# Two running sums seeded in PSUM, a second weight sum by DMA, and seven products in another order

## The chip, the cores and the metric

The kernel runs on one core of a Trainium2 chip. The metric is the device time of one execution in microseconds (us); of several executions the median is given. Engines are named as in the profile: PE is the matmul engine (TensorE), with its weight loads in rows of their own (PEld); DVE is the vector engine, ACT the scalar engine, POOL the engine that also issues DMAs which add to their destination, SP the one that issues the weight loads from memory. PSUM is the memory that PE writes, in eight banks of 128 x 512 float32.

## The reference: what is computed

One decoder block on 256 positions of width 2048, in float32: a half-step SwiGLU layer (width 5632), a token mixer (a recurrent branch and a short convolution that share one input projection, with one output projection), a second half-step SwiGLU layer, and a last norm.

```python
def swiglu_ffn(x, w_gate, w_up, w_down):
    return (jax.nn.silu(x @ w_gate) * (x @ w_up)) @ w_down
...
x = x + FFN_RESIDUAL_SCALE * swiglu_ffn(rms_norm(x, ffn1_norm[l]), ffn1_w_gate[l], ffn1_w_up[l], ffn1_w_down[l])
z = rms_norm(x, mix_norm[l]) @ w_in[l]
...
x = x + y @ w_out[l]
x = x + FFN_RESIDUAL_SCALE * swiglu_ffn(rms_norm(x, ffn2_norm[l]), ffn2_w_gate[l], ffn2_w_up[l], ffn2_w_down[l])
return rms_norm(x, final_norm)
```

All time goes to the large matrix products; their weights are about 340 MB, each read once.

## The kernel before

**Split operands.** A float32 product is made from parts: each operand is split into a high part `hi` (the value cast to the matmul's reduced type `fp32r`, by ACT, in two halves) and a low part `lo` (what is left, by DVE, one subtraction). A weight tile `raw` is 128 x 4 x 512 (1 MB); `parts_of` (L214) makes its `hi` and `lo`. A product of one weight tile with one row half of the activations is 12 matmuls in `multiply` (L228): 8 with `hi` (activation high and low), then 4 with `lo`. A "plain" piece makes both row halves at once: 24 matmuls, 16 with `hi`, then 8 with `lo`. The split tiles rotate over three slots (`split_tiles`, L198), so a cast waits until PE has done with the high part of the piece three places earlier.

**Blocks of seven products.** `seven` (L417) multiplies a 2 x 2 arrangement of activation tiles with a 2 x 2 arrangement of weight tiles (`w11`, `w12`, `w21`, `w22`) by seven products instead of eight, with sums of weights and sums of partial results. Beside these it adds plain pieces for the other activation tiles: `b2`, `b3` for one column half, `a2`, `a3` for the other. Four PSUM banks are in use, `a`, `c`, `e` and `d`. The products are numbered 0, 4, 5, 6, 2, 3, 1 in the order before, called `p0`, `p4` and so on here. `p0` goes to bank `a`, on which `p5`, `p6`, `a2` and `p3` go on adding; `p4` goes to `c`. After `p0` and `p4` ACT copies the banks to tiles in the on-chip memory (`snap`: `s1`, `s5`), and after `p5` and `p6` the running state of `a` (`u2`, `u3`). When a result is complete, `done` adds the copies to its bank on DVE (`total`, L871). Weight sums that `p4`, `p5` and `p3` need are made in `w11` by DVE (128 x 2048 each, three in a block); the one for `p6` is made in `w12` by a DMA that POOL issues and that adds `w22` to it (L464).

The kernel runs 28 such blocks: gate and up blocks by turns for five pairs of columns in each SwiGLU layer (`gate`, `up`; L867 on), a down block after the first, third and fifth pair (`down`, L793, with plain products of `product` before and after it), one in the input projection (`in_c`) and one in the output projection (`o_q`). The first gate block (its order is written out by hand) and `o_q` have paths of their own. Names in the profile carry `g`, `u`, `d`, `in_c`, `o_q` for these: `lo_u_p` is the low part of a weight tile of one of the seven products of an up block, `hi_u_x` the high part of a plain piece, `ps_u_c` the bank `c` of an up block.

**What sets the order.** Nearly everything is recorded through one helper at L43. Outside the opening and the end the program's order isn't kept as written: when the program is built, a planner goes through it with a clock of its own, and gives each engine the first instruction, in the order of writing, whose operands it believes ready. On the chip each engine then runs its list strictly in that order. The planner also gives out the tiles' slots; the weight loads are issued by SP as buffers come free. `raw` tiles have three buffers, `w11` and `w12` two of their own. The banks rotate over eight slots, in the order in which `bank` (L85) is called.

Of the kernel before, what the change touches and what calls it, by code (L numbers as in the profile page):

```python
# [13 lines left out]
ALU = mybir.AluOpType  # L14
AX = mybir.AxisListType

P = 128
D = 2048
S = 256
FF = 5632  # L20
NT = S // P
KD = D // P
KF = FF // P
CW = 512
NC_D = D // CW
UK = 4
# [23 lines left out]
def hybrid_block(ctx: ExitStack, tc: tile.TileContext, a: dict, out: bass.AP):  # L50
    nc = tc.nc
# [30 lines left out]
    work = ctx.enter_context(tc.tile_pool(name="work", bufs=2, side="right"))  # L82
    psum = ctx.enter_context(tc.tile_pool(name="psum", bufs=8, space=bass.MemoryType.PSUM))

    def bank(name):  # L85
        return psum.tile([P, 512], F32, tag="ps", name=name)

    def f32(ap):
        return ap.bitcast(F32)
# [13 lines left out]
    early = const.tile([P, 1], F32, name="early")  # L103
    act.activation(early, ones[:, :1], AF.Sqrt)

    idle = bank("idle")

    def keep_busy(n):
        for _ in range(n):
# [6 lines left out]
    def load_vectors(group, name, engine, after=None):  # L116
        n = sum(g[2] for g in group)
        rows = const.tile([n, P], F32, name=f"rows_{name}")
        cols = const.tile([P, n], F32, name=f"cols_{name}")
        at = 0  # L120
        if after is not None:
            engine.tensor_copy(rows[:, :1], after[:n, :1])
        for key, ap, k in group:
            engine.dma_start(rows[at : at + k, :], ap.rearrange("(r p) -> r p", p=P))
            vec[key] = cols[:, at : at + k]
            at += k

        def turn():
            pv = bank(f"pv_{name}")
            pe.transpose(pv[:, :n], rows, ident[:n, :n])  # L130
            dve.tensor_copy(cols, pv[:, :n])

        return turn
# [115 lines left out]
    class Norm:  # L249
# [12 lines left out]

        def transposed(self, k, src, whole):

            pt = bank(f"pt_{self.name}_{k}")[:, :S]
            for t in range(NT):
                pe.transpose(pt[:, t * P : (t + 1) * P], src[t], ident)
            g = self.gain[:, k : k + 1]
            hi, lo = whole[:, k % UK, :S], whole[:, k % UK, S:]
            parts = [  # L270
                lambda: act.activation(hi, pt, AF.Copy, scale=g),
                lambda: dve.scalar_tensor_tensor(lo, pt, g, f32(hi), op0=ALU.mult, op1=ALU.subtract),
            ]
            if self.exact is not None and k < 2 * UK:
                v = self.exact[:, k % UK, k // UK * S : (k // UK + 1) * S]
                parts.append(lambda: act.activation(v, pt, AF.Copy, scale=g))
            return parts
# [28 lines left out]

        def rows(self):

            pb = bank(f"pb_{self.name}")
            for t in range(NT):  # L310
                pe.matmul(pb[:, t * P : (t + 1) * P], ones, self.diag[t], start=True, stop=True)
            self.bc = work.tile([P, S], F32, tag="bc", name=f"bc_{self.name}")
            dve.tensor_copy(self.bc, pb[:, :S])
# [38 lines left out]
    def product(w, c, us, y, name, stagger=False, between=None):  # L352
        ps = [bank(f"ps_{name}_{t}") for t in range(NT)]
        cs = slice(c * CW, (c + 1) * CW)
        late = []
        for i, u in enumerate(us):
            blk = unit(w[u * UK * P : (u + 1) * UK * P, cs], f"{name}_{u}")
            begin, end = i == 0, i == len(us) - 1
            if stagger and i >= len(us) - 2:
                late.append((u, blk, begin, end))  # L360
            else:
                multiply([(ps[t], stationary(y(u), t), begin, end) for t in range(NT)], blk)
            if between:
                between(i)
            pump(1.5)

        for t in range(NT):
            for i, (u, blk, begin, end) in enumerate(late):
                if t < NT - 1:
                    multiply([(ps[t], stationary(y(u), t), begin, end)], blk)  # L370
                elif not end:
                    multiply([(ps[t], stationary(y(u), t), begin, i == len(late) - 2)], blk)
                else:
                    for o in (slice(0, CW // 2), slice(CW // 2, CW)):
                        ps.append(bank(f"ps_{name}_last")[:, : CW // 2])
                        multiply([(ps[-1], stationary(y(u), t), True, True)], [(h[:, o], l[:, o]) for h, l in blk])
        return ps

# [38 lines left out]
    def seven(w, rows, cols, sf, xs, name, keep, done, between=None, early=False, own=None, factor=None):  # L417
# [14 lines left out]
        def get(u, n, kept=False):  # L432
            src = w[u * UK * P : (u + 1) * UK * P, cols[n] : cols[n] + CW]
            return load(src, f"{name}_{u}{n}", kept=kept)
# [2 lines left out]
        w11, w12 = get(r0, 0, True), get(r0, 1, True)  # L437
        b2, w22 = get(xs[0][0], 1), get(r1, 1)
        b3 = get(xs[1][0], 1) if two else None
        a2, w21 = get(xs[0][0], 0), get(r1, 0)  # L440
        a3 = get(xs[1][0], 0) if two else None

        def snap(ps, n, scale=1.0):
# [7 lines left out]
        def usual(i, raw, n, *targets, first=None):  # L451
# [6 lines left out]
            if own and last:  # L458
                for t in range(NT):
                    own(t, n, apart[t, n])  # L460

        product_of(0, w11, a, True)
        dve.tensor_tensor(w11, w12, w11, op=ALU.add)
        nc.gpsimd.dma_start(w12, w22, accum_op=ALU.add)  # L464
# [3 lines left out]
        blk = None  # L468
# [55 lines left out]
    def ffn(tag, norm, after, opening=False):  # L524
        with tc.tile_pool(name=f"ffn{tag}", bufs=1, side="left") as fp:
# [10 lines left out]
            def turn_hidden(u, t, h, again):  # L536

                if u not in hidden:
                    hidden[u] = big(f"h{tag}_{u}")
                pt = bank(f"ph{tag}_{u}_{t}")  # L540
                for j in range(UK):
                    pe.transpose(pt[:, j * P : (j + 1) * P], h[:, j * P : (j + 1) * P], ident)
                pt = pt.rearrange("p (j c) -> p j c", j=UK)
                hi = hidden[u][:, :, t * P : (t + 1) * P]
                lo = hidden[u][:, :, S + t * P : S + (t + 1) * P]
                act.copy(hi, pt)
                dve.tensor_tensor(lo, pt, f32(hi), op=ALU.subtract)
                if again:
                    act.copy(quad(h), pt)
                    turned[u, t] = quad(h)  # L550
# [242 lines left out]
            def down(last):  # L793
# [24 lines left out]
                for c in (0, 3):  # L818
                    end = last and tag == 2 and c == NC_D - 1
                    ps = product(  # L820
                        wd, c, us[:-2] + [n, m], hidden.get, f"d{tag}_{m}_{c}", end,
                        (lambda i: settle()) if c == 0 else None,
                    )
                    Engine.pinned = end
                    if end:
                        finish(c, ps)
                    else:
                        for t in range(NT):
                            update(c, t, ps[t])
                    if c == 0:  # L830
                        sh = {}
                        two, last_sum, high, low = seven_of(
                            sh, hidden[m], hidden[n],
                            {(t, i): turned[u, t] for t in range(NT) for i, u in ((0, m), (1, n))},
                            quad(keep(f"hspare{tag}_{m}")),
                            [[quad(keep(f"hs{tag}_{m}_{i}_{z}", F32R)) for z in range(2)] for i in range(4)],
                        )
                        two()
                        high(5)
                        low(5)  # L840

                        def others(i):
                            if i == "sum":
                                high(6)
                                low(6)
                                last_sum()
                                high(2)
                                low(2)

                        got = {}  # L850

                        def add(t, b, ps, tiles):
                            got[t, b] = [ps] + tiles
                            if (0, b) in got and (1, b) in got:
                                for i in range(NT):
                                    update(2 - b, i, *got[i, b])

                        if tag == 1 and m == 5:
                            prepare()
                        seven(  # L860
                            wd, (m, n), (2 * CW, CW), sh, [(u, hidden[u]) for u in us[:-2]], f"d{tag}_{m}", keep, add,
                            others,
                        )
# [106 lines left out]
    with tc.tile_pool(name="mixer", bufs=1, side="left") as mp, tc.tile_pool(name="mixw", bufs=2, side="left") as mw:  # L970
# [35 lines left out]
        def gates(q):  # L1006
# [4 lines left out]
            th = {}  # L1011
            for g, hb in (("a", hba), ("i", hbi)):
                hi, lo = wgate[g]
                pg = bank(f"pgate_{g}_{q}")
                pe.matmul(pg[:, :S], hi[:, q, :], xs[:, :S], start=True, stop=False)
                pe.matmul(pg[:, :S], hi[:, q, :], xs[:, S:], start=False, stop=False)
                pe.matmul(pg[:, :S], lo[:, q, :], xs[:, :S], start=False, stop=True)
# [124 lines left out]
        def sc_c(between):  # L1142
# [10 lines left out]
            def turn(n):  # L1153
                for f in range(0, 4, 2):
                    pt = bank(f"pt_c{n}_{f}")
                    for i in range(2):
                        for t in range(NT):
                            o = i * S + t * P
                            pe.transpose(pt[:, o : o + P], z[t, n][:, (f + i) * P : (f + i + 1) * P], ident)
                    for i in range(2):  # L1160
                        q = 4 * (1 - n) + f + i
                        c = tmp("cc", q, S + 2, bufs=8)
# [79 lines left out]
        for g in range(2):  # L1242
            if g == 1:
                flush()
            ps = product(w_out, 0, (2 * g, 2 * g + 1), yT.__getitem__, f"o0_{g}")
            pst = bank(f"pst_{g}")
            for t in range(NT):
                pe.matmul(pst[:, t : t + 1], acc[:, g, t * P : (t + 1) * P], ones[:, :1], start=True, stop=True)
            tot = work.tile([P, NT], F32, tag="tot", name=f"tot_y{g}")
# [155 lines left out]
```

## Time and profile before

| | |
|---|---|
| median of 3 runs | 1726.82 us (1726.74 to 1728.6) |
| the profiled execution: its own time | 1726.91 us |
| the profiled execution: span from first to last instruction | 1725.1 us |
| DVE, instructions and busy time | 1212, 1452.2 us |
| ACT, instructions and busy time | 1406, 1077.8 us |
| data read from memory | 339.82 MB |

A group or timeline row reads: line, engine, operation, written tile `<-` read tiles, partitions x elements, and the count; a timeline row begins with its start and its length in us, and ends with the idle time before it and what ended that. The waits view lists who waited for whom, in us, times, and the longest. A row by stretches gives the stretch, its length, the busy time of PE, PEld, DVE, ACT and POOL with their instruction counts, the granted matmul clock, the busy share of the DMA engines and GB/s. Matmuls overlap: a row's length is that of the pipeline, and the time that one costs is read from start to start.

### The profile page before, as it was taken

How to read it: one execution, taken by the hardware profiler on the slowest of the kernel's cores; microseconds unless marked ns; L12 is line 12 of the kernel's file. 1: busy time of each engine (PE TensorE's matmuls, PEld its weight loads, DVE VectorE, ACT ScalarE, POOL GpSimd, SP SyncE). 2: the span in 40 equal slices, each digit the busy share in tenths (PEclk: the TensorE clock that was granted, in tenths of full speed). 3: DMA queues.
4: the chain of work that ended last, by engine and by line, in shares of the span. 5: the costliest groups of instructions: out<-in, count | busy, mean ns of one | idle time of the engine just before them, and what ended most of it. 6: DMA issues, size and time to landing. Idle time of an engine off the chain costs nothing.

```text
span 1725.1 us, 20426 instructions
## 1 busy us (share of the span) xinstructions
PE 1715.3 (99%) x7985; PEld 1432.9 (83%) x7985; DVE 1452.2 (84%) x1212; ACT 1077.8 (62%) x1406; POOL 35.3 (2%) x62
## 2 busy tenths in 40 slices
PE   9999999999999999999999999999999999999998
PEld 8888888888888888888888888888888888888886
DVE  7988889789789888787897889889788887788886
ACT  7666566656466656666965657655556664556664
POOL 0010000000000000000000000000000000000000
PEclk9999999999999999999999999999999999999999
DMA  8775777667677766655556675776777757677753
GB/s 300 225 258 174 242 234 227 214 236 233 182 238 226 227 201 219 211 160 193 175 197 205 204 251 165 228 237 224 230 227 219 244 171 243 214 225 220 254 179 128
DMA packets 178256, 372.59 MB, mean 216 GB/s; under 512 B 6132, under 2 KB 9072, under 8 KB 174448
## 3 DMA queue, kind: packets, MB, share of 16 engines
q1 hardware_dynamic: 173632, 340.81, 58.4%
q0 software_dynamic: 4352, 29.43, 8.5%
q8 instruction: 62, 1.02, 0.2%
q10 hardware_dynamic: 176, 1.06, 0.2%
q14 instruction: 34, 0.28, 0.0%
HBM read 339.82 MB, written 2.10 MB: 198 GB/s over the span
## 4 chain that ended last, share of the span: by engine, by line
PE 99%; DVE 0%; ACT 0%; DVEq 0%; issue 0%; ACTq 0%
PE ps_d L43 14%; PE ps_in L43 10%; PE ps_g_a L43 9%; PE ps_u_a L43 9%; PE ps_g_c L43 6%; PE ps_u_c L43 6%; PE ps_d_a L43 5%; PE ps_u_d L43 5%; PE ps_g_d L43 5%; PE ps_d_c L43 3%; PE ps_u_e L43 3%; PE ps_g_e L43 3%; PE ps_g L43 3%; PE ps_o L43 3%; PE ps_u L43 3%; PE ps_d_d L43 3%
## 5 line engine op out<-in xcount | busy, mean ns | idle before, releaser
L43 ACT CAST hi_g_p<-raw_g 128x1024 fp32r<-128x1024 f32 (+1 forms) x139 | 142.1, 1054 | 111.6 <-DVE raw_g L43 26.9
L43 DVE TENSOR_TENSOR lo_g_p<-raw_g,hi_g_p 128x2048 fp32r<-128x2048 f32 x70 | 159.8, 2289 | 42.3 <-ACT hi_g_p L43 41.6
L43 DVE TENSOR_TENSOR lo_u_p<-raw_u,hi_u_p 128x2048 fp32r<-128x2048 f32 x70 | 159.3, 2288 | 39.5 <-ACT hi_u_p L43 39.2
L43 ACT CAST hi_u_p<-raw_u 128x1024 fp32r<-128x1024 f32 x140 | 141.3, 1047 | 70.1 <-issue 23.1
L43 PE MATMUL ps_d<-hi_d,h 128*128 128x512 f32 x696 | 166.0, 390 | 0.0
L43 PEld LDWEIGHTS ps_d<-hi_d,h 128*128 128x128 f32 x696 | 130.0, 188 | 26.6
L43 ACT CAST hi_d<-raw_d 128x1024 fp32r<-128x1024 f32 x88 | 88.6, 1048 | 68.3 <-PE ps_u_d L43 19.9
L43 DVE TENSOR_TENSOR lo_d<-raw_d,hi_d 128x2048 fp32r<-128x2048 f32 x44 | 100.8, 2290 | 29.3 <-ACT hi_d L43 29.3
L43 PE MATMUL ps_in<-xT_nm,hi_in 128*128 128x512 f32 x512 | 122.5, 391 | 0.0
L43 ACT CAST hi_d_p<-raw_d 128x1024 fp32r<-128x1024 f32 x84 | 85.2, 1048 | 59.2 <-DVE raw_d L43 33.7
L43 PEld LDWEIGHTS ps_in<-xT_nm,hi_in 128*128 128x128 f32 x512 | 94.0, 188 | 18.8 <-ACT tha L43 0.5
L43 DVE TENSOR_TENSOR lo_d_p<-raw_d,hi_d_p 128x2048 fp32r<-128x2048 f32 x42 | 95.5, 2288 | 15.5 <-ACT hi_d_p L43 15.4
L43 ACT CAST hi_g_x<-raw_g 128x1024 fp32r<-128x1024 f32 (+1 forms) x79 | 81.2, 1058 | 42.9 <-PE ps_g_c L43 25.6
L43 ACT CAST hi_u_x<-raw_u 128x1024 fp32r<-128x1024 f32 x80 | 80.5, 1046 | 36.4 <-PE ps_u_c L43 22.1
L43 DVE TENSOR_TENSOR lo_g_x<-raw_g,hi_g_x 128x2048 fp32r<-128x2048 f32 x40 | 91.5, 2288 | 9.2 <-ACT hi_g_x L43 8.9
L43 DVE TENSOR_TENSOR lo_in<-raw_in,hi_in 128x2048 fp32r<-128x2048 f32 x32 | 73.2, 2288 | 26.7 <-ACT hi_in L43 26.3
L43 DVE TENSOR_TENSOR lo_u_x<-raw_u,hi_u_x 128x2048 fp32r<-128x2048 f32 x40 | 91.4, 2286 | 1.4 <-ACT hi_u_x L43 0.8
L43 PE MATMUL ps_d<-lo_d,h 128*128 128x512 f32 x348 | 86.2, 389 | 0.0
L43 ACT CAST hi_in<-raw_in 128x1024 fp32r<-128x1024 f32 x64 | 64.0, 1045 | 24.9 <-PE ps_in L43 15.2
L43 PEld LDWEIGHTS ps_d<-lo_d,h 128*128 128x128 f32 x348 | 65.3, 188 | 13.6
L43 DVE TENSOR_TENSOR raw_u<-raw_u,raw_u 128x2048 f32<-128x2048 f32 x30 | 68.7, 2289 | 8.5 <-DMA raw_u<-in_ffn_w_up_dram 8.1
L43 DVE TENSOR_TENSOR raw_g<-raw_g,raw_g 128x2048 f32<-128x2048 f32 x30 | 68.7, 2289 | 5.7 <-DMA raw_g<-in_ffn_w_gate_dram 5.2
(477 smaller groups left out, 3750.5 us busy)
## 6 DMA issues: line engine op xcount, KB each, us to landing
raw_d<-in_ffn_w_down_dram SPq DMA_DIRECT2D x88, 1024.0 KB, 5.2
raw_u<-in_ffn_w_up_dram SPq DMA_DIRECT2D x87, 1024.0 KB, 5.3
raw_g<-in_ffn_w_gate_dram SPq DMA_DIRECT2D x86, 1024.0 KB, 5.2
raw_in<-in_w_in_dram SPq DMA_DIRECT2D x32, 1024.0 KB, 5.1
raw_g<-raw_g POOLq DMA_DIRECT2D x10, 1024.0 KB, 7.0
raw_u<-raw_u POOLq DMA_DIRECT2D x10, 1024.0 KB, 7.0
raw_in_c<-in_w_in_dram SPq DMA_DIRECT2D x8, 1024.0 KB, 5.3
raw_o<-in_w_out_dram SPq DMA_DIRECT2D x8, 1024.0 KB, 5.2
```

The lines of the kernel that those rows point to most:

```text
L43: ins = getattr(self.engine, name)(*args, **kwargs)
```

## The change

`bank` notes for each new bank whether the one that had the slot before it was written as a whole by PE (`fit`). In `seven`, the 26 blocks without a path of their own get a new sequence.

- `p2` is made right after `p5`, ahead of the piece `b3`; `p6` comes behind `b3`. To match, `w21` is loaded ahead of `a2`, and in the down blocks the activation sums for `p2` are made before those for `p6` (`others`).
- The third weight sum, `w21` added to `w11` for `p3`, is made by a DMA of POOL in place of DVE.
- Where the slots of `c` and `d` fit, which is so in 21 of the 26 blocks (10 of the first layer, 11 of the second; not in `in_c`, nor in the first up block of either layer, the fourth gate block of the first and the first gate block of the second), the sums are seeded: `p4` is made first, into `e`, and ACT copies `e` to `c`; then `p0` into `a`, and ACT copies `a` to `d`. PE goes on adding on both, so that the snapshots `s1` and `s5` and the two DVE adds that used them fall away. `p0`'s weight tile is still split first, since the first weight sum overwrites it.

The transposes of hidden tiles and of `pt_c` are written as matmuls with the transpose flag, of which only the first of a bank starts it (`turn_into`); their number is the same.

```diff
+    written = [False] * 8
+    given = [0]
+    fit = {}
+
+    def bank(name, whole=True):
+
+        slot = given[0] % len(written)
+        given[0] += 1
+        fit[name] = written[slot]
+        written[slot] = whole
         return psum.tile([P, 512], F32, tag="ps", name=name)
+
+    def turn_into(ps, sources):
+
+        for i, src in enumerate(sources):
+            pe.matmul(
+                ps[:, i * P : (i + 1) * P], src, ident, is_transpose=True, start=i == 0, stop=True,
+                skip_group_check=True,
+            )
...
-        a2, w21 = get(xs[0][0], 0), get(r1, 0)
+        if early or own:
+            a2, w21 = get(xs[0][0], 0), get(r1, 0)
+        else:
+            w21, a2 = get(r1, 0), get(xs[0][0], 0)
...
+        if not early and own is None:
+            first = parts_of(w11, f"{name}_p0")
+            dve.tensor_tensor(w11, w12, w11, op=ALU.add)
+            nc.gpsimd.dma_start(w12, w22, accum_op=ALU.add)
+            seeded = fit[f"ps_{name}_c"] and fit[f"ps_{name}_d"]
+            if seeded:
+                product_of(4, w11, e, True)
+                act.copy(c, e)
+                product_of(0, None, a, True, blk=first)
+                act.copy(d, a)
+                s1, s5 = [], []
+            else:
+                product_of(0, None, a, True, blk=first)
+                product_of(4, w11, c, True)
+                s1, s5 = [snap(a, "s1")], [snap(c, "s5")]
+            if between:
+                between(0)
+            usual(0, b2, 1, (e, 1, not seeded, not two), (c, 0, False, False))
+            if between:
+                between(1)
+            dve.tensor_tensor(w11, w22, w11, op=ALU.add)
+            if between:
+                between("sum")
+            product_of(5, w11, a)
+            nc.gpsimd.dma_start(w11, w21, accum_op=ALU.add)
+            u2 = snap(a, "u2", -1.0)
+            if between:
+                between(2)
+            product_of(2, w22, c, end=not two)
+            if two:
+                usual(1, b3, 1, (e, 1, False, True), (c, 0, False, True))
+            done(0, 1, c, [u2])
+            product_of(6, w12, a)
+            u3 = snap(a, "u3", -1.0)
+            done(1, 1, e, [u3] + s5)
+            usual(0, a2, 0, (d, 0, not seeded, False), (a, 1, False, False))
+            product_of(3, w11, a, end=not two)
+            if two:
+                usual(1, a3, 0, (a, 1, False, True), (d, 0, False, False))
+            done(1, 0, a, [])
+            product_of(1, w21, d)
+            done(0, 0, d, s1)
+            return
...
                         def others(i):
                             if i == "sum":
-                                high(6)
-                                low(6)
                                 last_sum()
                                 high(2)
                                 low(2)
+                            elif i == 2:
+                                high(6)
+                                low(6)
```

More of the change, by code (lines that the diff above doesn't have):

```diff
@@ L83, in hybrid_block @@
     psum = ctx.enter_context(tc.tile_pool(name="psum", bufs=8, space=bass.MemoryType.PSUM))
-    def bank(name):
-        return psum.tile([P, 512], F32, tag="ps", name=name)
+    written = [False] * 8
[6 more added lines that the diff above has]
+        written[slot] = whole
+        return psum.tile([P, 512], F32, tag="ps", name=name)
+    def turn_into(ps, sources):
[4 more added lines that the diff above has]
+            )
     def f32(ap):
@@ L104, in hybrid_block @@
     act.activation(early, ones[:, :1], AF.Sqrt)
-    idle = bank("idle")
+    idle = bank("idle", False)
     def keep_busy(n):
@@ L128, in turn @@
         def turn():
-            pv = bank(f"pv_{name}")
+            pv = bank(f"pv_{name}", False)
             pe.transpose(pv[:, :n], rows, ident[:n, :n])
@@ L263, in transposed @@
         def transposed(self, k, src, whole):
-            pt = bank(f"pt_{self.name}_{k}")[:, :S]
+            pt = bank(f"pt_{self.name}_{k}", False)[:, :S]
             for t in range(NT):
@@ L307, in rows @@
         def rows(self):
-            pb = bank(f"pb_{self.name}")
+            pb = bank(f"pb_{self.name}", False)
             for t in range(NT):
@@ L374, in product @@
                     for o in (slice(0, CW // 2), slice(CW // 2, CW)):
-                        ps.append(bank(f"ps_{name}_last")[:, : CW // 2])
+                        ps.append(bank(f"ps_{name}_last", False)[:, : CW // 2])
                         multiply([(ps[-1], stationary(y(u), t), True, True)], [(h[:, o], l[:, o]) for h, l in blk])
@@ L540, in turn_hidden @@
                 pt = bank(f"ph{tag}_{u}_{t}")
-                for j in range(UK):
-                    pe.transpose(pt[:, j * P : (j + 1) * P], h[:, j * P : (j + 1) * P], ident)
+                turn_into(pt, [h[:, j * P : (j + 1) * P] for j in range(UK)])
                 pt = pt.rearrange("p (j c) -> p j c", j=UK)
@@ L1013, in gates @@
                 hi, lo = wgate[g]
-                pg = bank(f"pgate_{g}_{q}")
+                pg = bank(f"pgate_{g}_{q}", False)
                 pe.matmul(pg[:, :S], hi[:, q, :], xs[:, :S], start=True, stop=False)
@@ L1155, in turn @@
                     pt = bank(f"pt_c{n}_{f}")
[L1156 to L1159, printed above, removed]
+                    turn_into(
+                        pt, [z[t, n][:, (f + i) * P : (f + i + 1) * P] for i in range(2) for t in range(NT)]
+                    )
                     for i in range(2):
@@ L1245, in hybrid_block @@
             ps = product(w_out, 0, (2 * g, 2 * g + 1), yT.__getitem__, f"o0_{g}")
-            pst = bank(f"pst_{g}")
+            pst = bank(f"pst_{g}", False)
             for t in range(NT):
```

## The prediction

> **What bounds the kernel now.** I read the page first: the busy line, the chain, then the waits of the matmul engine (PE), then one table by stretches.
>
> ```profile
> span 1725.1 us, 20426 instructions
> ...
> PE 1715.3 (99%) x7985; PEld 1432.9 (83%) x7985; DVE 1452.2 (84%) x1212; ACT 1077.8 (62%) x1406; POOL 35.3 (2%) x62
> ...
> PE 99%; DVE 0%; ACT 0%; DVEq 0%; issue 0%; ACTq 0%
> ```
> ```profile
> PE idle L43 <- DVE ones L43: 1.1, 1, 1.1
> PE ps_g L43 <- ACT hi_g L43: 0.6, 1, 0.6
> 18.00:1717.00 1699.00, 1698.90 (x7908) 1418.99 (x7907) 1439.16 (x1185) 1063.47 (x1377) 34.63 (x56) 1.00 0.67 215
> 1717.00:1725.10 8.10, 0.00 (x0) 0.00 (x0) 2.67 (x10) 1.63 (x4) 0.00 (x0) 0.79 0.48 179
> ```
>
> PE is busy 1698.9 of the 1699 us between 18 and 1717 us, at the full granted clock; its two waits, 1.7 us together, are in the opening. So only two things can move the end: fewer matmuls, or a new pause of PE. The change has exactly as many matmuls as before (seven products of 12 and four plain pieces of 24 in a block with two more inputs, and the same transposes). It takes work from DVE, for which PE waits at no place but the start, and brings some operands closer to their due time. The question is where an operand now comes late.
>
> Here is the seam between a gate block and its up block, the first of its kind. PE, rows of 8 and 4 matmuls (`p3` low, `p0` high, `p0` low, `p4` high; then `p5`, `a2`, and `p3` low again):
>
> ```profile
> 232.09 1.07 PE L43 MATMUL ps_g_a<-lo_g_p,x 128*128 128x512 f32 x4
> ...
> 241.15 1.98 PE L43 MATMUL ps_u_a<-hi_u_p,x 128*128 128x512 f32 x8
> 242.97 1.07 PE L43 MATMUL ps_u_a<-lo_u_p,x 128*128 128x512 f32 x4
> 243.87 1.98 PE L43 MATMUL ps_u_c<-hi_u_p,xs 128*128 128x512 f32 x8
> ...
> 254.75 1.98 PE L43 MATMUL ps_u_e<-hi_u_x,x 128*128 128x512 f32 x8
> ...
> 265.63 1.98 PE L43 MATMUL ps_u_d<-hi_u_x,x 128*128 128x512 f32 x8
> ...
> 272.88 1.07 PE L43 MATMUL ps_u_a<-lo_u_p,x 128*128 128x512 f32 x4
> ```
>
> Eight matmuls take 1.82 us from start to start (242.97 - 241.15), one 0.227, a product of 12 2.72. What prepares them, ACT (casts of the high part, copies out of banks) and DVE (low parts, weight sums):
>
> ```profile
> 232.33 2.00 ACT L43 CAST hi_u_p<-raw_u 128x1024 fp32r<-128x1024 f32 x2 [1.63 <-issue]
> 237.72 0.60 ACT L43 ACTIVATE z<-ps_g_a 128x512 f32<-128x512 f32 x1 [3.40 <-PE ps_g_a L43]
> 239.07 2.00 ACT L43 CAST hi_u_p<-raw_u 128x1024 fp32r<-128x1024 f32 x2 [0.74 <-DVE raw_u L43]
> ...
> 246.88 0.59 ACT L43 ACTIVATE s_u<-ps_u_c 128x512 f32<-128x512 f32 x1
> ```
> ```profile
> 234.36 2.29 DVE L43 TENSOR_TENSOR lo_u_p<-raw_u,hi_u_p 128x2048 fp32r<-128x2048 f32 x1 [1.34 <-ACT hi_u_p L43]
> 236.69 2.29 DVE L43 TENSOR_TENSOR raw_u<-raw_u,raw_u 128x2048 f32<-128x2048 f32 x1
> 241.10 2.29 DVE L43 TENSOR_TENSOR lo_u_p<-raw_u,hi_u_p 128x2048 fp32r<-128x2048 f32 x1 [2.12 <-ACT hi_u_p L43]
> ...
> 250.65 4.49 DVE L43 TENSOR_TENSOR lo_u_p<-raw_u,hi_u_p 128x2048 fp32r<-128x2048 f32 x2
> ```
>
> This is a chain without a gap: `p0`'s cast starts 0.24 us after the last high product of the old block's `p3` (three split tiles are in rotation, so it waits for that tile), then its low part, the first weight sum, `p4`'s cast, `p4`'s low part, done at 241.10 + 2.29 = 243.39. Because it hangs on PE's own progress, less DVE work elsewhere does not make it earlier.
>
> **The change, part by part.**
>
> *`p4` ahead of `p0` (the 21 seeded blocks).* `p4`'s high products start at 241.15: cast halves are done at about 240.1 and 241.07, in time. Its low products are due where `p0`'s were, 242.97; the operand comes at 243.39. The price of a late operand is shown by PE's wait in the opening:
>
> ```profile
> 5.89 0.73 PE L43 MATMUL ps_g<-hi_g,xT_n 128*128 128x512 f32 x2 [0.58 <-ACT hi_g L43]
> ```
> ```profile
> 284.67 1.07 PE L43 MATMUL ps_g_a<-lo_g_p,x 128*128 128x512 f32 x4
> 285.58 0.62 PE L43 MATMUL ps_g_c<-hi_g_p,xs 128*128 128x512 f32 x2
> ...
> 1549.76 1.07 PE L43 MATMUL ps_g_a<-lo_g_p,x 128*128 128x512 f32 x4
> ...
> 1591.46 1.07 PE L43 MATMUL ps_u_a<-lo_u_p,x 128*128 128x512 f32 x4
> ```
>
> A pair after that wait takes 0.73 instead of 0.62: 0.11 more. So the low products would start 243.39 + 0.11 - 242.97 = 0.53 us late. The same seam is there in 8 seeded up blocks (last: the low part at 1589.59 against 1591.46 below) and, after an up block, in 4 gate blocks:
>
> ```profile
> 282.85 2.29 DVE L43 TENSOR_TENSOR lo_g_p<-raw_g,hi_g_p 128x2048 fp32r<-128x2048 f32 x1
> ...
> 1547.93 2.29 DVE L43 TENSOR_TENSOR lo_g_p<-raw_g,hi_g_p 128x2048 fp32r<-128x2048 f32 x1
> ...
> 1589.59 2.29 DVE L43 TENSOR_TENSOR lo_u_p<-raw_u,hi_u_p 128x2048 fp32r<-128x2048 f32 x1 [2.12 <-ACT hi_u_p L43]
> ```
>
> In those, 282.85 + 2.29 + 0.11 - 284.67 = 0.58 late. The other 9 seeded blocks follow a down product and have their operands earlier. Upper bound: 8 x 0.53 + 4 x 0.58 = 6.6 us. Lower bound 0, since the order on PE is made at build time by a planner that passes over a product whose operand its clock calls late. In the first down block it did so: four high products of `p2` stand between `p6`'s high and low ones.
>
> ```profile
> 167.43 1.07 PE L43 MATMUL ps_d_c<-hi_d_p,hs 128*128 128x512 f32 x4
> 168.33 2.08 PE L43 MATMUL ps_d_a<-hi_d_p,hs 128*128 128x512 f32 x8
> 170.25 0.62 PE L43 MATMUL ps_d_a<-lo_d_p,hs 128*128 128x512 f32 x2
> ```
>
> (Its first row is `p6`'s last four, the second is four of `p2` and more.) Here `p0` is ready and can fill. One matmul of it takes 0.23 off each pause, two leave 0.07 and 0.12, three close it. I take one, as the planner sees no reason for more when its clock is a little ahead of the chip: 8 x 0.30 + 4 x 0.35 = 3.8 us.
>
> [...]
>
> *Copies into `c` and `d` in place of the two snapshots.* Same count on ACT. No row writes a bank from a bank; the snapshot out of one is 0.59, and double that as the other bound still fits: `c` from `e` can start 0.29 us after `p4`'s end (246.88, `p4` ending at 246.59 here) and PE comes back to `e` one product, 2.72 us, later; a cast in flight (half of 2.00) may stand before it. Cost 0. `d` is needed 84 matmuls after its copy can start. The bank that `p4` now writes first is, in these blocks, the old block's `a`: emptied at 238.32 against 241.15. Cost 0.
>
> *Fewer DVE adds.* 26 weight sums at 2.29 and 42 adds of 128x512: 26 x 2.29 + 42 x 0.68 = 88 us of DVE's 1452:
>
> ```profile
> L43 DVE TENSOR_TENSOR s_g<-ps_g_d,s_g 128x512 f32<-128x512 f32 x10 | 6.8, 684 | 1.7 <-PE ps_g_d L43 1.7
> ```
>
> PE waits for none of it: gain 0.
>
> *The second accumulating DMA (26).*
>
> ```profile
> q1 hardware_dynamic: 173632, 340.81, 58.4%
> q0 software_dynamic: 4352, 29.43, 8.5%
> ...
> raw_u<-in_ffn_w_up_dram SPq DMA_DIRECT2D x87, 1024.0 KB, 5.3
> ...
> raw_u<-raw_u POOLq DMA_DIRECT2D x10, 1024.0 KB, 7.0
> ```
>
> 28 accumulates take 8.5% of the 16 DMA engines; 26 more bring 7.9%, from 0.67 to about 0.75 busy. It waits for `p5`'s low part (first of the pair at 250.65, done by 252.9); POOL has nothing else queued there. Landing at 259.9, cast 2.00 and low part 2.29: 264.2, due 272.88. Cover 8.7 us. Cost 0.
>
> *`p2` ahead of the second plain piece, `p6` behind it.* `p2` stands where that piece stood, 254.75, its low products 1.82 later at 256.57; its low part follows `p5`'s on DVE, 252.9 + 2.29 = 255.2. Cover 1.4. But `w22`'s buffer comes free only then, and `a2` now takes it: load issued 255.2, landed 260.5, first half cast by 261.5, due 265.63. Cover 4.1; in w_in's block, where DVE is fullest, I allow 0 to 2.3 us once and take 0. `u3`'s copy has 1.82 us until PE writes `a` again, needs 0.29 + 0.59, and a half cast of 1.0 before it makes it late by up to 0.1: 0 to 2.6 us over 26 blocks, 0 taken, as ACT is idle a third of the time.
>
> **Sum.** 1726.91 us is the profiled execution's own time (span 1725.1), 0.09 above the median 1726.82. 1726.9 + 3.8 = 1730.7.
>
> **Rivals.** 0.2%, 3.45 us, is about what measuring can tell from no change.
>
> *A, the forecast:* `p4`'s low operand late in 12 seams, one filling matmul or none: +3.8 to +6.6, 1730.7 to 1733.5. For it: the deficit stands in rows that repeat to 0.01 us. Against: the planner's order isn't in this trace.
>
> *B, not slower:* the planner puts two or more of `p0`'s matmuls in front: +0 to 8 x 0.07 + 4 x 0.12 = 1.0, so 1726.9 to 1727.9. It decides once two stand there. For it: the rows at 168.33.
>
> *C, `a2` or the accumulate late:* the load of `a2` shares the engines with the accumulate. It decides at a landing of 5.3 + 4.1 = 9.4 us; every 0.5 us beyond would cost 13 us in 26 blocks, 1739.9. Against: 7.0 is the accumulate's own landing and no load in these rows is near 9.
>
> *D, faster:* two adds of 0.68 less in the last down block could let the closing work begin earlier, 1.4 of the 8.1 us after PE: 1725.5. It would need 3.45, more than DVE's whole 2.67 there.
>
> *E, no change of order:* if the planner kept `p0` first, nothing would move: 1726.9.
>
> **How the numbers follow.** A 0.46, B 0.34, C 0.12, D 0.04, E 0.04. Slower is A and C, 0.58; same is B and E, 0.38; faster 0.04 for D and what I don't see. The likeliest is A at 1730.7; its own range is 1730.4 to 1736 (no filling, plus half of `u3`'s bound). The range for 8 in 10 runs from 1726.3, B with a little of D, to 1738, most of C.
>
> **What would show it.** PE rows: high rows of `p4` first in the up blocks, one or few of `p0` between them and `p4`'s low rows, then a pause of 0.3 us 12 times; the waits view should name DVE's `lo_u_p` and `lo_g_p` for PE. DVE busy should fall by about 88 us, q0's share rise to 16%, PE's busy time stay near 1715. The prediction is wrong if PE's stretch from 18 to 1717 us stays as long as it is, or if PE waits for a DMA or for ACT.

## The result and the profile after

The changed kernel takes 1750.06 us (median of 4 runs, 1746.86 to 1752.17); the kernel before, beside it, 1727.71 (1726.74 to 1729.05). The ratio is 1.0127, with a 95% interval from 1.0109 to 1.0145: 22.3 us slower. The forecast was 3.8 us slower, with a range that ended at +11.

The profiled execution of the changed kernel took 1752.17 us, the slowest of the four, so its rows hold some 2 us more than the median. From its page, the busy line, the chain and the line of the queue of accumulating DMAs (packets, MB, share of 16 engines):

```profile
span 1750.4 us, 20467 instructions
...
PE 1724.7 (99%) x7985; PEld 1433.7 (82%) x7985; DVE 1374.5 (79%) x1144; ACT 1079.2 (62%) x1406; POOL 57.8 (3%) x88
...
q0 software_dynamic: 8096, 56.70, 16.6%
...
PE 84%; DMA 6%; DVE 5%; ACT 3%; issue 2%; ACTq 0%; DVEq 0%; POOLq 0%; POOL 0%
```

The chain was 99% PE before. Now 6% of it is DMA, about 105 us, and PE's share is 84%: the chain passes through transfers in many places. That share is no price, since most of a transfer is covered by other work; what is lost is read from PE's pauses. PE's count of matmuls is the same. The waits of PE (who waited, for whom; total, times, longest):

```profile
PE ps_d_a L43 <- ACT u_d L43: 5.8, 4, 1.9
PE ps_u_e L43 <- DVE lo_u_p L43: 2.5, 8, 0.3
PE ps_u_a L43 <- ACT u_u L43: 2.4, 2, 1.9
PE ps_in_c_d L43 <- ACT hi_in_c_x L43: 1.5, 1, 1.5
PE ps_g_e L43 <- DVE lo_g_p L43: 1.4, 4, 0.4
PE ps_in_c_a L43 <- ACT d_snap L43: 1.1, 1, 1.1
...
```

There are two families and one row apart. Rows with DVE's `lo_u_p` and `lo_g_p` are the forecast's seams: 8 and 4 times, as named. Rows with ACT's copies of bank `a` (`u_d`, `u_u`, and `d_snap` in the input projection) are the step that the forecast put at 0. The row apart is `hi_in_c_x`: there PE waits for the cast of `a2`'s weight tile, which landed late.

How much each family costs is read from PE's start-to-start times: a 512-column matmul has 0.227 us (eight take 1.82), and whatever is more is a pause or a slow matmul. The sum of the excess, over all starts more than 0.24 us apart, was 4.6 us before and is 28.8 after. Of the 24.2 more, 7.2 lie at the 12 seams (8 x 0.48, 4 x 0.52, and 0.11 more on each next matmul), 9.6 at the second target of `a2`, which waits for `u3`'s copy, in seven blocks, 2.9 in the input projection, and 3.2 are slow matmuls behind two of the long pauses. The small rest is for the most part the 0.11 behind the other pauses.

**A seam.** PE, then DVE, in the first seeded up block:

```profile
246.71 1.98 PE L43 MATMUL ps_u_e<-hi_u_p,xs 128*128 128x512 f32 x8
249.00 1.20 PE L43 MATMUL ps_u_e<-lo_u_p,xs 128*128 128x512 f32 x4 [0.31 <-DVE lo_u_p L43]
```
```profile
246.65 2.29 DVE L43 TENSOR_TENSOR lo_u_p<-raw_u,hi_u_p 128x2048 fp32r<-128x2048 f32 x1 [2.12 <-ACT hi_u_p L43]
```

The low products were due at 246.71 + 1.82 = 248.53 and started at 249.00. Nothing of `p0` stands between `p4`'s high and low rows.

**A late copy of `u3`.** The first down block: the accumulate in the chain (start, length), ACT, PE.

```profile
168.51 8.25 DMA raw_d<-raw_d
```
```profile
176.86 2.94 ACT L43 CAST hi_d_p<-raw_d 128x1024 fp32r<-128x1024 f32 x3 [3.29 <-DMA raw_d<-raw_d]
179.71 0.59 ACT L43 ACTIVATE u_d<-ps_d_a 128x512 f32<-128x512 f32 x1
```
```profile
175.82 1.07 PE L43 MATMUL ps_d_a<-lo_d_p,hs 128*128 128x512 f32 x4
176.72 1.97 PE L43 MATMUL ps_d_d<-hi_d_x,h 128*128 128x512 f32 x8
180.35 2.14 PE L43 MATMUL ps_d_a<-hi_d_x,h 128*128 128x512 f32 x8 [1.65 <-ACT u_d L43]
```

PE had finished `p6` in bank `a` at about 176.7, and the copy could have started at 177.0 (0.29 us after the end of the product, as the snapshot at 246.88 in the kernel before). But ACT's list has the cast for `p3` first, and that one waits 3.29 us for the accumulate to land, at 176.76. Three half casts later the copy starts, at 179.71. The first target of `a2` takes 1.82 us, so PE was due in bank `a` at 178.54 and started at 180.35.

**A late load does the same.** The last down block: from the chain, the load of `a2`; then ACT.

```profile
1688.86 9.07 DMA raw_d<-in_ffn_w_down_dram
```
```profile
1698.03 2.00 ACT L43 CAST hi_d_x<-raw_d 128x1024 fp32r<-128x1024 f32 x2 [7.02 <-DMA raw_d<-in_ffn_w_down_dram]
1699.93 1.99 ACT L43 CAST hi_d_p<-raw_d 128x1024 fp32r<-128x1024 f32 x2
1701.82 1.04 ACT L43 CAST hi_d_x<-raw_d 128x1024 fp32r<-128x1024 f32 x1
1702.77 0.59 ACT L43 ACTIVATE u_d<-ps_d_a 128x512 f32<-128x512 f32 x1
```

This load takes 9.07 us, where the group's median before was 5.2. It was issued 1.74 us behind a second accumulate (at 1687.12), and ACT stands before it for 7.02 us, with the copy queued behind.

### The profile page after: what moved, and what is told of

Its sections match the earlier page's. It is cut to its first block, busy times and chain, and to the rows that moved or that the text cites. A ratio compares the mean times of both kernels' runs of the same rounds, so it can differ in the third digit from the quotient of the medians.

```text
span 1750.4 us, 20467 instructions
## 1 busy us (share of the span) xinstructions
PE 1724.7 (99%) x7985; PEld 1433.7 (82%) x7985; DVE 1374.5 (79%) x1144; ACT 1079.2 (62%) x1406; POOL 57.8 (3%) x88
## 4 chain that ended last, share of the span: by engine, by line
PE 84%; DMA 6%; DVE 5%; ACT 3%; issue 2%; ACTq 0%; DVEq 0%; POOLq 0%; POOL 0%
PE ps_d L43 12%; PE ps_in L43 10%; PE ps_g_a L43 9%; PE ps_u_a L43 9%; PE ps_g_c L43 5%; PE ps_g_d L43 4%; PE ps_u_d L43 4%; PE ps_d_a L43 4%; PE ps_u_c L43 4%; PE ps_g_e L43 4%; PE ps_u_e L43 3%; PE ps_o L43 3%; PE ps_g L43 3%; PE ps_u L43 2%; PE ps_d_d L43 2%
## 5 line engine op out<-in xcount | busy, mean ns | idle before, releaser
L43 DVE TENSOR_TENSOR lo_d_p<-raw_d,hi_d_p 128x2048 fp32r<-128x2048 f32 x42 | 95.7, 2288 | 25.2 <-ACT hi_d_p L43 25.1
L43 PEld LDWEIGHTS ps_in<-xT_nm,lo_in 128*128 128x128 f32 x512 | 65.6, 191 | 2.5
L43 PE MATMUL ps_in<-xT_nm,lo_in 128*128 128x256 f32 x512 | 66.4, 283 | 0.0
```

The costliest lines, as they stand in the source:

```text
L43: ins = getattr(self.engine, name)(*args, **kwargs)
```

## The experiments

Times are medians; the kernel before ran beside each group at 1727.5 to 1727.8. Two theories to begin with: T1, the second accumulate lands late and holds ACT's list, so `u3`'s copy is late; T2, `p4` first makes 12 short pauses. Two rivals to T1: T3, `p6` behind `b3` leaves `u3`'s copy too short a time, whoever makes the sum; T4, not the wait for the sum costs the time but the accumulate's traffic, which makes loads late.

**The third sum back on DVE.**

```diff
-            nc.gpsimd.dma_start(w11, w21, accum_op=ALU.add)
...
+            dve.tensor_tensor(w11, w21, w11, op=ALU.add)
             product_of(3, w11, a, end=not two)
```


> The changed kernel with the third weight sum back on DVE, where it stood before; the rest kept. Two theories share the 22 us between before (1727.7) and after (1750.1). T1: the second accumulate lands late (9 us instead of 7), ACT stands in its list before the cast that needs it, and u3's copy behind that cast is late for PE; pauses of seven u3 copies 9.6 us, in_c 2.9, slow matmuls after the longest pause 1.6, together 14. T2: p4's low part is late in 12 seams, 12 x 0.6 = 7.2 us. T1 and T2 together expect here 1750.1 - 14 = 1736, the PE pauses before bank a gone, 12 short pauses for DVE's low parts left. T3, the rival to T1: p6 behind p2 leaves u3's copy only 1.82 us, whoever makes the sum; then the pauses before bank a stay and the time is 1748 to 1750.

Measured: 1736.8 (1734.9 to 1737.7), 1.005 of before [1.0033, 1.0067]. PE's waits:

```profile
PE ps_u_e L43 <- DVE lo_u_p L43: 2.5, 8, 0.3
PE ps_g_e L43 <- DVE lo_g_p L43: 1.5, 4, 0.4
PE idle L43 <- DVE ones L43: 1.1, 1, 1.1
PE ps_d_e L43 <- DVE lo_d_p L43: 0.4, 1, 0.4
PE ps_g L43 <- ACT hi_g L43: 0.2, 1, 0.2
```

Every wait for ACT's copies is gone; the seams are left, with one more in a down block. T3 falls: the window of 1.82 us for `u3` is enough when no accumulate runs. The second accumulate costs 1750.1 - 1736.8 = 13.3 us here. This doesn't say yet by which way.

**No block seeded.**

```diff
-            seeded = fit[f"ps_{name}_c"] and fit[f"ps_{name}_d"]
+            seeded = False
```


> The changed kernel with no block seeded: p0 first into a, p4 into c, the snapshots s1 and s5 and their DVE adds are back; second accumulate and new order of p2 and p6 kept. T2 expects the 12 short pauses for DVE's low parts gone and the pauses before bank a unchanged: 1750.1 - 7.2 = 1743. If the short pauses are only where a lateness of the accumulate shows up, or if PE would lose the time elsewhere, it stays at 1748 to 1750.

Measured: 1761.7 (1758.3 to 1764.7), 11.6 us slower than the change instead of 7.2 faster. PE's waits:

```profile
PE ps_u_a L43 <- ACT u_u L43: 8.5, 4, 2.1
PE ps_d_a L43 <- ACT u_d L43: 8.0, 5, 2.2
...
```

The seams did go: no row for `lo_u_p` or `lo_g_p` is left. But the copies of `u3` in these two rows are now late by 16.5 us in nine places, against 8.2 in six. ACT waits 25.1 us, four times, for loads of `hi_u_x` (3.4 before this edit). A kernel with the accumulate in it isn't a ground on which another part can be priced by taking it away.

**On ACT, `u3`'s copy ahead of `p3`'s cast.**

```diff
...
-            product_of(3, w11, a, end=not two)
+            with tc.issue_after(taken["u3"].ins):
+                blk3 = parts_of(w11, f"{name}_p3")
+            product_of(3, None, a, end=not two, blk=blk3)
```


> The changed kernel with one thing told to the planner: on ACT the cast of the accumulated tile for p3 stands behind u3's copy. The accumulate, its traffic and its landing are the same. T1, as a matter of ACT's order, expects the pauses before bank a gone (9.6 us in seven blocks and 1.3 in in_c, and 1.6 of slow matmuls): 1737 to 1738. T1 as a matter of the landing itself (the sum comes too late for p3) expects PE to wait for p3's cast instead: 1745 to 1750. T3 (the short window of u3 alone) expects some 1748 to 1750.

`taken` holds the instruction of the copy. Measured: 1749.4 (1748.9 to 1751.0): no gain. PE's waits:

```profile
PE ps_u_e L43 <- DVE lo_u_p L43: 6.5, 8, 1.2
...
PE ps_d_a L43 <- ACT u_d L43: 1.7, 2, 0.9
...
```

The late copies shrank from 8.2 to 1.9 us (with 0.2 in an up block), so ACT's order was what made them late. But the wait at the up blocks' seams grew from 2.5 to 6.5 us. The likely reason, which no run tests by itself: `p3`'s cast now stands behind that copy in every block, also where the sum had long landed, and `p4`'s operands of the next block come later. The time moved to another place; a change of ACT's order alone doesn't take the loss away.

**The accumulate alone, in the kernel before.**

```diff
         product_of(5, w11, a)
+        by_dma = not early and own is None
+        if by_dma:
+            nc.gpsimd.dma_start(w11, w21, accum_op=ALU.add)
...
-        dve.tensor_tensor(w11, w21, w11, op=ALU.add)
+        if not by_dma:
+            dve.tensor_tensor(w11, w21, w11, op=ALU.add)
```


> The kernel before with one part of the change alone: the third weight sum made by an accumulating DMA, issued after p5 as in the change; p6 ahead of p2, no seeds. If the late accumulate costs its 14 us in any order: 1741 to 1742. If it costs only together with the short window that p6 behind b3 leaves to u3's copy (before, p2 stands between p6 and a2, so the copy has 2.72 us more), nearly nothing: 1727.5 to 1730.

Measured: 1791.0 (1788.4 to 1791.7), 63.5 us slower than before; both expectations missed. From POOL's waits, and PE's:

```profile
POOL raw_u L492 <- DMA raw_u<-in_ffn_w_up_dram: 160.7, 9, 20.4
```
```profile
PE ps_u_a L43 <- ACT hi_u_p L43: 11.4, 4, 3.3
PE ps_g_a L43 <- ACT u_g L43: 7.5, 7, 2.0
PE ps_d_a L43 <- ACT u_d L43: 6.9, 5, 5.0
...
```

Here `w21` is loaded behind `a2`; POOL waits for that load in nine of ten up blocks, the sum comes too late for `p3` itself (first row of PE), and the copies are late too. In the changed kernel, where `w21` is loaded ahead of `a2`, the same accumulate costs 13.3 us. The load order is the likely reason for the difference; no run changed it alone.

**The seams filled by hand.**

```diff
-                product_of(4, w11, e, True)
-                act.copy(c, e)
-                product_of(0, None, a, True, blk=first)
...
+                highs(e, 4, p4, range(UK))
+                highs(a, 0, first, (0, 1))
+                lows(e, 4, p4)
+                act.copy(c, e)
+                highs(a, 0, first, (2, 3))
+                lows(a, 0, first)
                 act.copy(d, a)
```


> The changed kernel with four of p0's high matmuls written between p4's high and low ones in the seeded blocks, so that PE has 0.9 us of ready work where it waited 0.5; nothing else differs. T2 (p4's low part late in 12 seams) expects these pauses gone and the rest as it was: 1750.1 - 6.5 = 1743.6. If a seam's pause only gives time to something that is late further on (the accumulate, u3's copy), the time comes back there: 1748 to 1750.

`highs` and `lows` write the matmuls of a product's high and low part. Measured: 1745.9 (1744.6 to 1747.0), 4.2 us less than the change. The first seeded up block on PE:

```profile
246.58 1.98 PE L43 MATMUL ps_u_e<-hi_u_p,xs 128*128 128x512 f32 x8
248.39 1.07 PE L43 MATMUL ps_u_a<-hi_u_p,x 128*128 128x512 f32 x4
249.30 1.07 PE L43 MATMUL ps_u_e<-lo_u_p,xs 128*128 128x512 f32 x4
```

All 12 pauses are closed. The waits for ACT's copies are as large as in the changed kernel (8.7 us in seven places; there 8.5 in seven).

**The order alone; and seeds with filled seams, with the sum on DVE.** The first is the two edits "sum on DVE" and "no block seeded" together, the second "sum on DVE" and "seams filled".

> The third weight sum on DVE and no block seeded: what is left of the change is the order (p2 before b3, p6 behind it, w21's load before a2's) and the transposes as matmuls. If the accumulate (13.3, from the run with the sum on DVE) and p4 first (6.5 to 7.1) are all of it: 1736.8 - 7 = 1729.5 to 1730.5, with no pause of PE for u3's copy. If the order has a cost of its own (w22's buffer free later, a2's load late, DVE as full as before): 1733 to 1740, with PE waits for ACT's hi parts of the plain pieces.

> Seeds kept with four of p0's high matmuls between p4's high and low ones, third sum on DVE, new order kept. Both theories expect nearly the time of before: 1727.5 plus at most 1 to 2, so 1728 to 1730. If the copies from bank to bank cost PE something (c is needed 1.81 us after p4's end here instead of 2.72), PE waits for ACT's ps_u_c and the like, 21 blocks by 0.1 to 0.5: 1731 to 1738.

Measured: 1728.1 (1726.5 to 1729.5), ratio 1.0001 [0.9992, 1.0011]; and 1727.9 (1727.3 to 1729.2), ratio 1.0000 [0.9991, 1.0009]. PE's waits in the second:

```profile
PE idle L43 <- DVE ones L43: 1.1, 1, 1.1
PE ps_d_e L43 <- ACT ps_d_c L43: 0.6, 1, 0.6
PE ps_g L43 <- ACT hi_g L43: 0.5, 1, 0.5
```

The new order is free, and the copies from bank to bank cost one wait of 0.6 us. So, as far as these runs can tell, the change's loss is the accumulate and the seams, and nothing else. Neither variant is faster than the kernel before, and there is no room for it: in both PE is as full as it was there.

**The accumulate runs, and nobody waits for it.**

```diff
-            product_of(3, w11, a, end=not two)
+            product_of(3, w12, a, end=not two)
```


> The changed kernel, but p3 is made from w12's tile instead of the accumulated w11 (p3 is then a wrong product; all instructions and transfers are the same in number and size). The second accumulate still runs and still reads w21 and writes w11; only nobody waits for its landing. T1 as a wait (ACT stands before p3's cast until the landing) expects the 13 us gone: 1736 to 1738. T4, the rival: it is the transfer's traffic (it shares the DMA engines with the loads, so a2's load comes late, and SP waits for it before w21's buffer is loaded again): then 1745 to 1750, with ACT waiting for loads.

This kernel leaves out the use of the third sum: `p3` reads `w12`'s tile, with as many instructions and transfers of the same size. Measured: 1745.4 (1742.8 to 1745.9): the wait is worth 4.7 us here, and 8.6 of the accumulate's 13.3 remain with nobody waiting for it. T4 takes the larger part. One thing isn't separated: `w12`'s tile is now in use until `p3`, which can hold back the next load into its buffer. ACT's waits for loads:

```profile
ACT hi_d_x L43 <- DMA raw_d<-in_ffn_w_down_dram: 16.5, 5, 7.2
ACT hi_d L43 <- DMA raw_d<-in_ffn_w_down_dram: 16.4, 5, 3.4
...
ACT hi_in_c_x L43 <- DMA raw_in_c<-in_w_in_dram: 7.0, 2, 6.4
```

The pauses of the last down block (2.2 us) and of the input projection (3.4 us) are still there, and what ACT waits for in front of them is loads.

**The seams filled, and nobody waits for the accumulate.** The two edits together.

> Two edits together on the changed kernel: four of p0's high matmuls between p4's high and low ones, and p3 made from w12's tile instead of the accumulated w11 (a wrong product, the same work), so that the second accumulate runs and nobody waits for it. What is left to cost anything is the transfer beside the loads: 31 loads issued within 5 us of a second accumulate took 9.5 us to land, the others 5.2. T4 (traffic makes a2's load and in_c's loads late) expects 1745.4 - 4.2 to 6.5 = 1739 to 1741, ACT waiting for loads. If the wait for the sum and the seams are all: 1728 to 1731.

Measured: 1735.8 (1735.0 to 1736.7), 3 us under the expectation, since filling was worth 9.5 us here. What is left over the 1727.9 without an accumulate, 7.9 us, is the traffic by itself, but for the longer use of `w12`. PE's waits:

```profile
PE ps_d_a L43 <- ACT u_d L43: 2.1, 1, 2.1
PE ps_in_c_d L43 <- ACT hi_in_c_x L43: 1.5, 1, 1.5
PE ps_in_c_a L43 <- ACT d_snap L43: 1.1, 1, 1.1
...
```

**Half the size.** With the seams filled, the DMA adds two of the four slices of the tile, DVE the other two.

```diff
-            nc.gpsimd.dma_start(w11, w21, accum_op=ALU.add)
+            nc.gpsimd.dma_start(w11[:, :2], w21[:, :2], accum_op=ALU.add)
...
+            dve.tensor_tensor(w11[:, 2:], w21[:, 2:], w11[:, 2:], op=ALU.add)
```


> The changed kernel with the filled seams (1745.9), and the second accumulate of half the size: two of the four slices of the tile are added by the DMA, two by DVE before p3 (1.15 us there). If lateness grows with the transfer's length and everything has a cover of some us (half the transfer holds a load back by 2 us instead of 4, and lands earlier itself): the 18 us left over before are nearly gone, 1728 to 1732. If the cost goes with the number of accumulates that run beside the loads, not with their length: 1741 to 1746. In proportion it would be 1737.

Measured: 1730.0 (1728.3 to 1732.5), ratio 1.0011 [1.0002, 1.0021]. Half the transfer costs 2.1 us where the whole cost 18. The view of the accumulate's line in this kernel, and of the same line in the changed kernel:

```profile
DMA to landing us min/median/max: 4.8/5.7/9.1
```
```profile
DMA to landing us min/median/max: 8.1/9.0/12.0
```

So the cost isn't in proportion to the bytes. It fits lateness that counts only beyond a cover: a median landing of 5.7 us is hidden nearly everywhere, one of 9.0 isn't. No size between the two was run. Put together:

| the second accumulate | seams as in the change | seams filled |
|---|---|---|
| none, sum on DVE | 1736.8 | 1727.9 |
| half of it | | 1730.0 |
| runs, nobody waits | 1745.4 | 1735.8 |
| runs, `p3` waits | 1750.1 | 1745.9 |

## Why the prediction was wrong

- **Direction and bound.** "Slower" was right, but for the smaller part of the loss: 13.3 of the 22.3 us come from a term that the sum put at 0. "Only two things can move the end: fewer matmuls, or a new pause of PE" held in the main: 24.2 of the 25.3 us between the two spans are pauses and slow matmuls. The slow ones, 3.2 us, are a third thing that the sentence left out.
- **`p4` ahead of `p0`: right, its size taken at the wrong end.** The 12 seams are the ones named, the late operand is the one named, and a pause with its 0.11 is 0.59 and 0.63 against 0.53 and 0.58 worked out. The assumed filling matmul wasn't there: the planner put none between, so the rows give 7.2 instead of 3.8, a little above the upper bound of 6.6. By medians the seams are worth 8.9 without the accumulate.
- **Copies from bank to bank: right.** In the run that put `u3` first the row of a copy is 0.58 long, as the snapshot's; PE waits for it once, 0.6 us.
- **Fewer DVE adds: gain 0 was right,** and DVE's busy time fell by 77.7 us instead of 88. Added up one by one, DVE's instructions are 88.7 us shorter (1519.4 before, 1430.8 after); the busy time counts overlapping rows once, and there is less overlap now.
- **The second accumulate, "Cover 8.7 us. Cost 0.": the step that failed.** Its cost was 13.3 us with the seams as they are and 18 with the seams filled. It was priced by the rows of the first accumulate, 7.0 us. In the kernel before only 1 of 325 weight loads is issued within 5 us of the start of one of those, and that in the opening. The second one runs beside the loads of `a2` and what follows, and takes 9.0, and those loads come late by it: with nobody waiting for the sum, 8.6 of the 13.3 us remain. The other 4.7 are the wait for the sum. Its own reader was safe all the same: it landed 7 us or more before `p3` began in every block. What was not counted is that both waits, for the sum and for the late loads, stand in ACT's list, with work of others behind them. The part on added waits asked only when `p3` was due, and not who is queued behind the waiting cast.
- **`u3`'s copy, "0 taken, as ACT is idle a third of the time": the same failure seen from the other side.** Only half a cast was put ahead of it, 0.1 us. In the two blocks shown, ACT's idle time is spent at the head of its list, 3.29 us before the accumulate and 7.02 before the load; a copy behind that can't use it. It was up to 2.06 us late.
- **`a2`'s load, cover 4.1, and rival C: the collision was named, the way it costs for the most part not.** C said that it decides at a landing of 9.4 us, and priced it in 26 blocks. In 24 of them `a2`'s load was issued ahead of the second accumulate, and PE didn't wait for it. It was issued behind it in the last down block, where it landed after 9.1 us, and in the input projection, where it took 10.0. Only there did it go as C has it: PE waits 1.5 us for `hi_in_c_x`. In the last down block `a2`'s cast was still in time, and what came late was the copy behind it in ACT's list. The two loads behind the accumulate in the input projection, and the accumulate:

```profile
raw_in_c<-in_w_in_dram SPq DMA_DIRECT2D x2, 1024.0 KB, 10.2
raw_in_c<-raw_in_c POOLq DMA_DIRECT2D x1, 1024.0 KB, 9.3
```

(The transfers of the changed kernel issued from 753 to 758 us; before, the same two loads took 5.2.) Against C stood "no load in these rows is near 9", and that was a statement about rows in which no accumulate ran beside a load.
- **The range.** Its upper end took in "most of C" at 11 us. C and the wait on ACT together were 13 to 18.

What stays open: filling the seams is worth 8.9 us with the sum on DVE, 9.5 when nobody waits, and 4.2 by medians with the wait. The runs of the changed kernel lie 5.3 us apart, which may be a part of it; no run here separates the rest. Nor was it settled why the planner orders ACT's list so that more copies are late in the unseeded kernel.

## What to carry to other kernels

A transfer's price is read from rows in which it ran beside the same traffic as it will; a landing time from a quiet stretch (here 7.0 us, against 9.0 beside loads) is too low. When an operation gets a slower source, ask on which engine its reader waits and what is queued behind that reader, since an engine that runs its list in order passes the wait on to operands that have nothing to do with it, as ACT did in the first down block: it stood 3.29 us before the sum, and PE got `u3`'s copy 1.81 us late. A cover of a few us can hide nearly the whole cost up to its edge: here half the size, which landed after 5.7 us (the whole after 9.0 in the changed kernel), cost a ninth.

## What the runs showed of the hardware that was not expected

An accumulating DMA within on-chip memory and a load from memory slowed each other here. In the changed kernel 30 weight loads were issued in the 5 us from the start of a second accumulate; their median landing was 9.7 us (8.4 to 11.7), that of the loads issued at other times 5.4. With half the accumulate the medians of all loads of up and gate tiles were 5.8 and 5.7 us, against 6.3 and 6.2 in the changed kernel and 5.3 and 5.2 before. The second accumulate, beside these loads, takes 9.0 us, and the first one of the same kernel, with hardly a load behind it, 7.0. Both are stretched; how they share is shown by no run here.

A pause of about 2 us was followed by slow matmuls in two places, and in two it was not. The four longest pauses before bank `a`, 2.0, 1.8, 1.9 and 2.1 us in this order, each followed over 5 us in a table by stretches of the changed kernel (the seventh figure behind the stretch is the granted clock):

```profile
123.30:128.30 5.00, 4.98 (x15) 3.93 (x16) 4.96 (x6) 2.75 (x3) 0.00 (x0) 0.66 0.68 222
180.30:185.30 5.00, 4.95 (x22) 4.06 (x23) 5.00 (x5) 2.93 (x3) 0.00 (x0) 1.00 1.04 383
1204.50:1209.50 5.00, 5.00 (x22) 4.15 (x23) 5.00 (x5) 2.89 (x3) 0.00 (x0) 1.00 1.05 388
1703.40:1708.40 5.00, 4.99 (x15) 3.95 (x16) 5.00 (x6) 2.41 (x6) 0.00 (x0) 0.66 0.63 210
```

Twice the clock is 0.66 and 15 matmuls begin where 22 do otherwise: 7 x 0.227 = 1.6 us on top of the pause. The clock fell behind the pauses of 2.0 and 2.1 us, and not behind those of 1.8 and 1.9. But length alone doesn't decide: with the seams filled, a pause of 2.3 us in the last down block was followed by the full clock.

```profile
1697.40:1702.40 5.00, 4.99 (x22) 4.14 (x23) 5.00 (x6) 2.42 (x6) 0.00 (x0) 1.00 0.68 210
```

What decides it stays open.
